# The output projections' weights of a two-layer trunk: split by two GpSimd transfers instead of a ScalarE copy and a VectorE subtraction

## Chip, cores and metric

One NeuronCore of a Trainium2 chip runs the whole kernel. The metric is device time in microseconds (us); each kernel was run several times and the median counts. Besides, one execution was taken by the hardware profiler; all rows below are from it.

## What is computed

Two residual layers on 256 tokens of width 1024, in float32. Layer 0 is a sparse attention mixer with three branches (compressed, selected, windowed), layer 1 a sliding-window attention with a sink. Cut to what matters here:

```python
for i in range(2):
    h = rms_norm(x, norm_gains[i])
    q, k, v, ..., z = split(h @ w_in)          # projections of the layer
    o = attention(q, k, v, ...)                # 16 heads of 64
    x = x + (o * silu(z)) @ w_out              # w_out: 1024 x 1024
```

The change concerns the last line of each layer, the product with `w_out` (`a_w_out` in layer 0, `b_w_out` in layer 1).

## The kernel before, in words

TensorE works in a reduced float32 format (F32R). To keep the accuracy of float32, each operand is written as a high part, its value rounded to F32R, and a low part, the value minus the high part. A product then takes three matmuls: high by high, high by low, low by high (`wh` and `wl` are the parts of a weight, `oz[h][:, 0]` and `oz[h][:, 1]` those of the gated attention output of token half h).

Every weight matrix is cut into pieces of 512 KB (128 partitions x 2 x 512 elements, or other shapes of nearly that size). `load_w` (L172) handles one piece: `load_raw` (L145) issues one transfer from HBM on SyncE's queue (L149) into a tile `wraw`; `split_w` (L152) then makes `wh` with a rounding copy (mostly on ScalarE, L141) and `wl` with a subtraction on VectorE (L169). There are five buffers each for `wraw`, `wh` and `wl`. `wraw` comes free as soon as the split is done; `wh` and `wl` only when the last matmul that reads the piece has run.

`out_proj` (L454) takes eight pieces of `w_out`, called (kk, n): kk is a quarter of the 1024 rows, n a half of the columns. Its order is written out (L462): first kk 0 to 2 for both n and both token halves h, then kk 3. Sums for n = 0 lie in the PSUM tiles `pya`, for n = 1 in `pyb`; the very last quarter of the output (layer 1, h = 1, n = 1) is cut in two, `pyb` and `tail`. Rows kk of `w_out` meet the heads of attention unit kk, so that the matmuls of kk can run as soon as unit kk is through with attention (`finish_unit`, L418); kk 3 waits for the last unit.

Nothing in the program fixes the order of the instructions across helpers: a planner puts each engine's instructions in order when the kernel is built, by a priority (program order, raised by `tc.high_priority(offset=...)`, which is HP = 200 for the splits) and by its own forecast of when operands and buffers are ready. So the pieces of `w_out` are loaded and split long before `out_proj` stands in the program, among the attention units, and its matmuls fill gaps of TensorE there. Each engine then works its list strictly in order.

GpSimd has work of its own that the attention waits for: in each unit the probabilities `p` are scaled by L71, eight instructions for h = 1 in layer 0, after VectorE has made their factor `rg`, and before TensorE transposes them (L447). The rest of GpSimd's work are sums of the rotary terms (L66), the gate (L405, L406) and small tables.

Of the kernel before, what the change touches and what calls it, by code (L numbers as in the profile page):

```python
# [20 lines left out]
F32 = mybir.dt.float32  # L21
F32R = mybir.dt.float32r
# [3 lines left out]
ALU = mybir.AluOpType  # L26
# [7 lines left out]
EPS = 1e-6  # L34
NEG = -1e30
HP, HPZ, HPS, HPT, HPQ, HPF = 200, 200, 0, 100, 250, 0
HPC, HPK = 300, 250
RSC, QLO = 'p', 'd'
WPS = ('d', 'd', 'd', 'd', 'd', 'd', 'd', 'd', 'd')
PHASES = (4, 13, 23, 29, 37, 43, 49, 55)  # L40
# [50 lines left out]
def tile_hybrid_trunk(ctx: ExitStack, tc: tile.TileContext, x, positions, norm_gains, a_w_in, a_cmp_pos,  # L91
                      a_cmp_w2, a_w_out, b_w_in, b_w_out, small, cmp_w1, out):
    nc = tc.nc
    pool = Pool(nc.gpsimd)
# [6 lines left out]
    wpool = ctx.enter_context(tc.tile_pool(name="wpool", bufs=NWHL))  # L101
# [8 lines left out]
    def banks(name, tag="acc"):  # L110
        return [bank(f"{name}{h}", tag) for h in range(2)]

    def mm(o, l, r, start, stop):
        nc.tensor.matmul(o, lhsT=l, rhs=r, start=start, stop=stop)  # L114
# [18 lines left out]
    nload, NLOW = [0], 4  # L133
# [5 lines left out]
    def copy_to(eng, dst, src):  # L139
        if eng == 'a':  # L140
            nc.scalar.activation(dst, src, AF.Copy)  # L141
        else:
            ENG[eng].tensor_copy(dst, src)

    def load_raw(w, k0, nk, c0, n, step=None):  # L145
        raw = wpool.tile([128, nk, n], F32, name="wraw", tag="wraw", bufs=NRAW)
        for k in range(0, nk, step or nk):
            ks = slice((k0 + k) * 128, (k0 + k + (step or nk)) * 128)
            nc.sync.dma_start(raw[:, k:k + (step or nk)], w[ks, c0:c0 + n].rearrange("(k p) n -> p k n", p=128))  # L149
        return raw  # L150

    def split_w(raw, step=None):  # L152
        wh = wpool.tile(list(raw.shape), F32R, name="wh", tag="wh")
        wl = wpool.tile(list(raw.shape), F32R, name="wl", tag="wl")
        with tc.high_priority(offset=HP if nload[0] >= NLOW else 0):
            hp_ = WHS[sum(nload[0] >= n for n in PHASES)]
            for k in range(0, raw.shape[1], step or raw.shape[1]):
                ks = slice(k, k + (step or raw.shape[1]))
                copy_to(hp_[nload[0] % len(hp_)], wh[:, ks], raw[:, ks])
            pat = WPS[sum(nload[0] >= n for n in PHASES)]  # L160
            eng = pat[nload[0] % len(pat)]
            nload[0] += 1
            cut = {'d': raw.shape[1], 'p': 0, 'b': raw.shape[1] // 2}[eng]
            cuts = [(nc.vector, slice(0, cut)), (pool, slice(cut, raw.shape[1]))]
            if step:
                cuts = [((nc.vector, pool)[k >= cut], slice(k, k + 1)) for k in range(raw.shape[1])]
            for e_, ks in cuts:
                if ks.stop > ks.start:
                    e_.tensor_tensor(wl[:, ks], raw[:, ks], wh[:, ks].bitcast(F32), op=ALU.subtract)  # L169
        return wh, wl  # L170

    def load_w(w, k0, nk, c0, n):  # L172
        return split_w(load_raw(w, k0, nk, c0, n))

    xt0 = work.tile([128, 2, D], F32, name="x", tag="big", bufs=1)
    xh = [xt0[:, h] for h in range(2)]
# [277 lines left out]
    def out_proj(oz, w, xt, sq_out, last):  # L454

        ws = {}
        pys = [banks("pya", "acc"), banks("pyb", "s")]
        acc = [[pys[n][h] for n in range(2)] for h in range(2)]
        KM = 3
        if last:  # L460
            tail = ps_a.tile([128, 256], F32, name="tail", tag="pz")
        order = [(kk, n, h) for n in range(2) for kk in range(KM) for h in range(2)]  # L462
        order += [(kk, n, h) for h in range(2) for n in range(2) for kk in range(KM, 4)]
        for kk, n, h in order:
            if (kk, n) not in ws:
                ws[kk, n] = load_w(w, 2 * kk, 2, 512 * n, 512)
            wh, wl = ws[kk, n]
            for k in range(2):
                sh, sl = oz[h][:, 0, 2 * kk + k, :], oz[h][:, 1, 2 * kk + k, :]
                if last and h == 1 and n == 1:  # L470
                    continue
                for i, (s, m) in enumerate(((sh, wh), (sh, wl), (sl, wh))):
                    mm(acc[h][n], s, m[:, k, :], kk == 0 and k == 0 and i == 0, kk == 3 and k == 1 and i == 2)
            if last and h == 1 and n == 1:

                for q in range(2):
                    for k in range(2):
                        sh, sl = oz[h][:, 0, 2 * kk + k, :], oz[h][:, 1, 2 * kk + k, :]
                        for i, (s, m) in enumerate(((sh, wh), (sh, wl), (sl, wh))):
                            mm(tail if q else acc[h][n][:, 0:256], s, m[:, k, 256 * q:256 * q + 256],  # L480
                               kk == 0 and k == 0 and i == 0, kk == 3 and k == 1 and i == 2)
            if kk == 3:
                sl_ = slice(512 * n, 512 * (n + 1))
                if last:
                    for c0, c1, src in (((512, 768, acc[h][n][:, 0:256]), (768, 1024, tail)) if h == 1 and n == 1
                                        else ((512 * n, 512 * n + 512, acc[h][n]),)):
                        nc.vector.tensor_tensor(xt[h][:, c0:c1], src, xt[h][:, c0:c1], op=ALU.add)
                        nc.sync.dma_start(outd[h * 128:(h + 1) * 128, c0:c1], xt[h][:, c0:c1])
                else:
                    nc.vector.tensor_tensor(xt[h][:, sl_], acc[h][n], xt[h][:, sl_], op=ALU.add)  # L490
                    sq = work.tile([128, 512], F32, name="xsq", tag="sq", bufs=1)
                    nc.scalar.activation(sq, xt[h][:, sl_], AF.Square, accum_out=sq_out[:, n, h:h + 1])
# [86 lines left out]
    def queries(n):  # L579
        acc = banks("aq")  # L580
        for kk in range(4):
            w = load_w(awi, 2 * kk, 2, 512 * n, 512)
            for h in range(2):
                proj(acc[h], hT, h, w, 2, 2 * kk)
        q_prep([heads(acc[h]) for h in range(2)], 0, qTs, 8 * n, r0, nrq0)

    with tc.tile_pool(name="cmp", bufs=1) as cp:
# [8 lines left out]
        for kk in range(4):  # L596
            w = split_w(first_w[kk], 1 if kk < FK else None) if kk < len(first_w) else load_w(awi, 6, 2, 1024, 512)
# [197 lines left out]
    sqs = work.tile([128, 2, 2], F32, name="sqs1", tag="sqs")  # L795
    xh = load_x("x1")
    out_proj(ozs, awo, xh, sqs, False)
    hT = work.tile([128, 2, 8, T], F32R, name="hT1", tag="hT", bufs=1)
    with tc.high_priority(offset=200):
# [73 lines left out]
    for step in 'q0 k0 z0 a0 q1 z1 a1 z2 a2 z3 a3'.split():  # L873
        {'q': queries1, 'k': lambda n: keys1(), 'z': zs1, 'a': attend1}[step[0]](int(step[1:]))
    out_proj(ozs, bwo, xh, None, True)


# [31 lines left out]
```

## Time and profile before

| | us |
|---|---|
| median of 3 runs | 289.76 (289.17 to 291.66) |
| the profiled execution's own time | 289.89 |
| its span, first to last instruction | 288.10 |
| outside of the span (289.89 less 288.10) | 1.79 |
| TensorE busy (share of the span) | 271.3 (94%) |
| VectorE busy | 221.1 (77%) |
| ScalarE busy | 184.2 (64%) |
| GpSimd busy | 124.3 (43%) |

Matmuls overlap in TensorE's pipeline, so that its 94% does not mean that it could take no more work. A chain of waits is the work that ended last, followed back step by step to what released it; time of an instruction counts for the end only where it is on that chain. In the rows PE is TensorE, PEld its weight loads, DVE VectorE, ACT ScalarE, POOL GpSimd, SP SyncE.

### The profile page before, as it was taken

Reading aid. Unit: us, or ns where it says so; the run is one execution under the profiler, and the core shown is the slowest. Engines: PE = TensorE matmul, PEld = TensorE weight load, DVE = VectorE, ACT = ScalarE, POOL = GpSimd, SP = SyncE. Lnnn points to the kernel's source line nnn. Section 1 sums busy time; section 2 is a strip of 40 time slices with the busy share of each in tenths; the row PEclk is TensorE's granted clock in tenths of the full one; section 3 lists DMA queues with packets and bytes.
Section 4 is the critical chain, followed back from the end, with each engine's and each line's share of the span. In section 5 each row is a group of like instructions: output and inputs, shape, how many; then the busy total and the mean of one; then the engine's idle time right before and its main releaser. Section 6 shows DMA issues by size and latency. Waiting matters only on the chain.

```text
span 288.1 us, 5292 instructions
## 1 busy us (share of the span) xinstructions
PE 271.3 (94%) x1772; PEld 229.1 (80%) x1772; DVE 221.1 (77%) x621; ACT 184.2 (64%) x441; POOL 124.3 (43%) x182
## 2 busy tenths in 40 slices
PE   5898999998999799998998999999999799999995
PEld 3667988877898797876776877789989799877874
DVE  3798847579769998988698284989969988784533
ACT  5491974365666767889688473547666949783620
POOL 7494514477720583636252500034394392253200
PEclk9799999999999999999999999999999989999999
DMA  7988769145527544221102354137774423100003
GB/s 224 306 265 262 256 224 245 49 138 147 146 75 200 165 149 146 76 74 36 39 0 75 147 167 127 47 99 220 221 213 154 141 78 104 45 2 0 1 2 146
DMA packets 33115, 37.52 MB, mean 130 GB/s; under 512 B 1680, under 2 KB 21568, under 8 KB 32960
## 3 DMA queue, kind: packets, MB, share of 16 engines
q1 hardware_dynamic: 33088, 37.18, 42.5%
q8 instruction: 14, 0.23, 0.3%
q14 instruction: 13, 0.11, 0.1%
HBM read 36.13 MB, written 1.05 MB: 129 GB/s over the span
## 4 chain that ended last, share of the span: by engine, by line
PE 71%; DVE 15%; ACT 5%; issue 3%; DMA 3%; SPq 1%; POOL 1%; ACTq 0%
PE pz L114 12%; PE po L114 8%; PE aqb L114 7%; PE pyb L114 6%; PE pya L114 6%; PE aq L114 5%; PE ptp L447 5%; DVE wl L169 4%; PE aks L114 4%; DMA wraw<-in_a_w_in_dram 3%; PE s L114 3%; PE avw L114 2%; PE sb L114 2%; DVE p L414 2%; PE akw L114 2%
## 5 line engine op out<-in xcount | busy, mean ns | idle before, releaser
L169 DVE TENSOR_TENSOR wl<-wraw,wh 128x1024 fp32r<-128x1024 f32 (+2 forms) x64 | 79.3, 1245 | 13.6 <-ACT wh L141 12.9
L141 ACT ACTIVATE wh<-wraw 128x1024 fp32r<-128x1024 f32 (+3 forms) x58 | 59.6, 1031 | 29.7 <-PE avw L114 4.9
L114 PE MATMUL pz<-hT,wh 128*128 128x256 f32 x256 | 50.3, 291 | 1.9 <-DVE zt L400 1.9
L114 PEld LDWEIGHTS pz<-hT,wh 128*128 128x128 f32 x256 | 41.4, 194 | 2.2 <-ACT sq L310 2.1
L114 PE MATMUL pz<-hT,wl 128*128 128x256 f32 x128 | 36.8, 287 | 0.0
L71 POOL TENSOR_SCALAR p<-p,rg 128x256 f32<-128x256 f32 (+1 forms) x48 | 22.9, 495 | 29.6 <-DVE rg L768 15.3
L416 ACT ACTIVATE p<-p,nm 128x128 f32<-128x128 f32 (+1 forms) x64 | 28.4, 447 | 4.9 <-DVE nm L414 4.7
L66 POOL TENSOR_TENSOR rt<-rt,rt 128x512 f32<-128x512 f32 (+2 forms) x14 | 21.3, 1530 | 23.8 <-DVE rt L324 23.8
L141 ACT ACTIVATE ptsb<-ptp 128x512 f32<-128x512 f32 x36 | 20.7, 586 | 10.4 <-PE ptp L447 10.4
L114 PEld LDWEIGHTS pz<-hT,wl 128*128 128x128 f32 x128 | 24.8, 194 | 0.0
L414 DVE CUSTOM_DVE_ANT_0 p<-s,mask,nrq 128x128 f32<-128x128 f32 (+1 forms) x64 | 24.2, 407 | 0.0
L114 PE MATMUL aqb<-wh,hT 128*128 128x512 f32 x64 | 21.3, 396 | 0.0
L114 PE MATMUL s<-kt,qT 128*128 128x272 f32 (+1 forms) x96 | 19.6, 305 | 1.6 <-DVE cwide L741 0.7
L114 PE MATMUL aq<-wh,hT 128*128 128x512 f32 x64 | 20.6, 393 | 0.0
L71 POOL TENSOR_SCALAR pb<-pb,rg 128x128 f32<-128x128 f32 (+1 forms) x24 | 13.8, 591 | 15.4 <-DVE rg L865 9.8
L414 DVE CUSTOM_DVE_ANT_0 pb<-sb,mask,nsink 128x128 f32<-128x128 f32 (+1 forms) x32 | 13.8, 471 | 5.1 <-PE ptp L447 3.9
L114 PEld LDWEIGHTS s<-kt,qT 128*128 128x128 f32 x96 | 14.5, 189 | 3.3 <-PE s L114 1.2
L447 PE MATMUL ptp<-identr,p 128*128 128x128 f32 x96 | 15.6, 277 | 1.5 <-ACT ptsb L141 1.4
L416 ACT ACTIVATE pb<-pb,nm 128x128 f32<-128x128 f32 (+1 forms) x32 | 14.2, 446 | 2.6 <-DVE nm L414 2.5
L114 PE MATMUL akc<-wh,hT 128*128 128x512 f32 x32 | 12.3, 451 | 3.0 <-ACT hT L280 1.2
L447 PEld LDWEIGHTS ptp<-identr,p 128*128 128x128 f32 x96 | 11.3, 140 | 3.6 <-ACT ptsb L141 2.1
L114 PEld LDWEIGHTS aq<-wh,hT 128*128 128x128 f32 x64 | 11.9, 188 | 2.5 <-ACT sq L310 0.2
(250 smaller groups left out, 689.5 us busy)
## 6 DMA issues: line engine op xcount, KB each, us to landing
wraw<-in_a_w_in_dram SPq DMA_DIRECT2D x25, 512.0 KB, 4.6
wraw<-in_b_w_in_dram SPq DMA_DIRECT2D x18, 512.0 KB, 4.3
wraw<-in_a_w_out_dram SPq DMA_DIRECT2D x8, 512.0 KB, 3.7
wraw<-in_b_w_out_dram SPq DMA_DIRECT2D x8, 512.0 KB, 4.0
x<-in_x_dram SPq DMA_DIRECT2D x4, 256.0 KB, 3.5
w<-in_cmp_w_dram SPq DMA_DIRECT2D x1, 1024.0 KB, 6.7
x<-in_x_dram SPq DMA_DIRECT2D x2, 512.0 KB, 3.8
wraw<-in_a_w_in_dram SPq DMA_DIRECT2D x2, 456.0 KB, 4.3
```

What stands on the lines that cost most here:

```text
L66: self.eng.tensor_tensor(out, a, b, op=op)
L71: self.eng.tensor_scalar(out, a, s0, s1, op0=op0, op1=op1)
L114: nc.tensor.matmul(o, lhsT=l, rhs=r, start=start, stop=stop)
L141: nc.scalar.activation(dst, src, AF.Copy)
L169: e_.tensor_tensor(wl[:, ks], raw[:, ks], wh[:, ks].bitcast(F32), op=ALU.subtract)
L414: nc.vector.tensor_tensor_reduce(out=p, in0=s, in1=mk, scale=nr, scalar=floor, op0=ALU.add, op1=ALU.min, accum_out=nm)
L416: nc.scalar.activation(p, p, AF.Exp, scale=-1.0, bias=nm, accum_out=total)
L447: nc.tensor.transpose(pt[:, i], s, ident)
```

## The change

`out_proj` calls a new function `load_parts` instead of `load_w`. For each of its 16 pieces (8 per layer) GpSimd issues three things: a transfer from HBM straight into `wh`, which rounds on its way since the target's type is F32R; an instruction that writes the negative of `wh` into `wl`; and a second transfer of the same 512 KB that is added to what `wl` holds. `wraw`, the copy on ScalarE and the subtraction on VectorE are gone for these pieces. The three are raised in priority by HPD = 250 in place of 200. The count `nload`, by which the engines of the other splits are chosen, still moves by one for each piece. All other weights stay as they were.

```diff
-HPC, HPK = 300, 250
+HPC, HPK, HPD = 300, 250, 250
@@
+    def load_parts(w, k0, nk, c0, n):
+
+        src = w[k0 * 128:(k0 + nk) * 128, c0:c0 + n].rearrange("(k p) n -> p k n", p=128)
+        wh = wpool.tile([128, nk, n], F32R, name="wh", tag="wh")
+        wl = wpool.tile([128, nk, n], F32R, name="wl", tag="wl")
+        with tc.high_priority(offset=HPD):
+            nload[0] += 1
+            nc.gpsimd.dma_start(wh, src)
+            pool.tensor_scalar(wl, wh.bitcast(F32), -1.0, 1.0, op0=ALU.mult, op1=ALU.mult)
+            nc.gpsimd.dma_start(wl, src, accum_op=ALU.add)
+        return wh, wl
@@ out_proj
             if (kk, n) not in ws:
-                ws[kk, n] = load_w(w, 2 * kk, 2, 512 * n, 512)
+                ws[kk, n] = load_parts(w, 2 * kk, 2, 512 * n, 512)
```

## Rows read from the trace of the kernel before

**Rows 1.** The page's head and its first part: busy us, share, instructions.

```profile
span 288.1 us, 5292 instructions
PE 271.3 (94%) x1772; PEld 229.1 (80%) x1772; DVE 221.1 (77%) x621; ACT 184.2 (64%) x441; POOL 124.3 (43%) x182
```

**Rows 2.** The page's chain that ended last, by engine, as shares of the span.

```profile
PE 71%; DVE 15%; ACT 5%; issue 3%; DMA 3%; SPq 1%; POOL 1%; ACTq 0%
```

**Rows 3.** Busy time by stretch (from:to, length, engines, PEclk, DMA share, GB/s).

```profile
95.00:118.00 23.00, 20.97 (x167) 19.37 (x166) 21.71 (x74) 16.98 (x47) 14.12 (x18) 1.00 0.43 139
...
137.00:166.00 29.00, 27.71 (x177) 21.81 (x178) 19.69 (x97) 19.97 (x65) 10.55 (x24) 1.00 0.19 63
...
227.00:251.00 24.00, 22.04 (x171) 20.42 (x170) 19.90 (x62) 18.06 (x55) 12.92 (x17) 0.93 0.28 88
251.00:285.00 34.00, 33.97 (x208) 27.00 (x206) 20.24 (x62) 16.88 (x49) 8.19 (x14) 1.00 0.05 17
```

**Rows 4.** The chain in order of time, 110 to 152 us (start, us, what).

```profile
116.67 1.16 DVE wl L169
...
120.41 1.14 DVE wl L169
...
133.21 1.38 DVE wl L169
...
148.86 0.95 ACT wh L141
```

**Rows 5.** Groups by shape: line, operation, count, busy us, mean ns, idle before.

```profile
L169 DVE TENSOR_TENSOR wl<-wraw,wh 128x1024 fp32r<-128x1024 f32 x59 | 74.4, 1267 | 11.9 <-ACT wh L141 11.3
L141 ACT ACTIVATE wh<-wraw 128x1024 fp32r<-128x1024 f32 x53 | 55.8, 1055 | 24.0 <-PE aks L114 3.9 <-PE pya L114 3.8 <-PE pz L114 3.6
```

**Rows 6.** Tile `wraw`: issue ns (min/median/max), first to last start; time to landing.

```profile
L149 SPq DMA_DIRECT2D wraw<-in_a_w_in_dram x30: 367/368/1556, 2.1 to 86.9; - x30
...
L149 SPq DMA_DIRECT2D wraw<-in_a_w_out_dram x8: 367/368/371, 88.7 to 111.9; - x8
...
DMA to landing us min/median/max: 3.0/4.1/8.7
```

**Rows 7.** VectorE in order of time: the splits of `w_out`, first and last per layer.

```profile
102.09 1.22 DVE L169 TENSOR_TENSOR wl<-wraw,wh 128x1024 fp32r<-128x1024 f32 x1
...
165.95 2.49 DVE L169 TENSOR_TENSOR wl<-wraw,wh 128x1024 fp32r<-128x1024 f32 x2
...
230.53 1.22 DVE L169 TENSOR_TENSOR wl<-wraw,wh 128x1024 fp32r<-128x1024 f32 x1
...
272.49 1.23 DVE L169 TENSOR_TENSOR wl<-wraw,wh 128x1024 fp32r<-128x1024 f32 x1 [1.93 <-ACT wh L141]
```

**Rows 8.** ScalarE in order of time: the last copy of each layer's `w_out`, its wait.

```profile
164.86 1.06 ACT L141 ACTIVATE wh<-wraw 128x1024 fp32r<-128x1024 f32 x1 [0.28 <-PE pya L114]
...
271.40 1.06 ACT L141 ACTIVATE wh<-wraw 128x1024 fp32r<-128x1024 f32 x1 [1.73 <-PE pyb L114]
```

**Rows 9.** TensorE in order of time: uses of those pieces, and its last matmul.

```profile
173.30 0.40 PE L114 MATMUL pyb<-wl,oz 128*128 128x512 f32 x1
...
280.88 0.39 PE L114 MATMUL pyb<-wl,ozb 128*128 128x512 f32 x1
...
284.69 0.28 PE L114 MATMUL tail<-wh,ozb 128*128 128x256 f32 x1
```

**Rows 10.** GpSimd in order of time (start, us, line, operation, idle before).

```profile
13.34 1.81 POOL L77 TENSOR_SCALAR wh<-wraw 128x1024 fp32r<-128x1024 f32 x1 [0.18 <-DMA wraw<-in_a_w_in_dram]
...
101.61 0.62 POOL L405 TENSOR_SCALAR zth<-zth 128x512 f32<-128x512 f32 x1 [3.92 <-ACT zth L401]
102.31 2.16 POOL L406 TENSOR_TENSOR zt<-zth,zt 128x512 f32<-128x512 f32 x1
...
113.90 4.89 POOL L71 TENSOR_SCALAR p<-p,rg 128x256 f32<-128x256 f32 x8 [4.40 <-DVE rg L768]
...
122.16 1.28 POOL L406 TENSOR_TENSOR zt<-zth,zt 128x512 f32<-128x512 f32 x1
```

## The prediction

> **What bounds the kernel now.** I read the page first. No engine is the plain bound: TensorE's 94% are busy time with overlapping matmuls, VectorE has 77%, ScalarE 64%, GpSimd 43% [rows 1]. So the next view is the chain that ended last: 71% TensorE, 15% VectorE, 5% ScalarE, 1% GpSimd [rows 2]. The reader should take from it that an edit which relieves VectorE and ScalarE can give back at most what lies on their fifth of the chain, and that GpSimd, which gets the new work, is nearly absent from it now.
>
> Then the stretches in which the splits of `w_out` run. In layer 0 the eight subtractions start between 102.09 and 165.95 us, in layer 1 between 230.53 and 272.49 us [rows 7]. VectorE is busy 21.71 of 23.00 us from 95 to 118, and 19.69 of 29.00 from 137 to 166; in layer 1 it is busy 19.90 of 24.00 from 227 to 251, and from 251 to 285 TensorE is busy 33.97 of 34.00 [rows 3]. So layer 0 has a VectorE that the attention queues for, and layer 1's end has TensorE in the way whatever the others do.
>
> The chain in order of time says which splits count. In layer 0 four pieces of it are splits of `w_out`: three subtractions of 1.16, 1.14 and 1.38 us and one copy of 0.95 us [rows 4], together 4.63 us. In layer 1, behind 230 us, the chain's long pieces hold no split of `w_out` at all; they are matmuls and transposes. The other twelve subtractions already hide behind TensorE.
>
> **What is removed.** 16 subtractions of 1.267 us are 20.3 us of VectorE, 16 copies of 1.055 us are 16.9 us of ScalarE [rows 5]; off SyncE's queue go 16 issues of 0.368 us [rows 6], which stood on no engine that computes. Of these 37 us only the 4.63 on the chain are sure to come off. Taking them off can't gain less than zero and, if VectorE's whole queue in layer 0 moves up, gives at most its eight subtractions, 8 x 1.267 = 10.1 us. I take 4.6: by the chain the rest is hidden by matmuls that stay.
>
> **What is added on GpSimd.** Each piece brings one negation and two issues. The nearest row for the negation is the rounding copy of the same shape on GpSimd, 1.81 us, from below twice the 0.62 us of the half-size one-input instruction, 1.24 [rows 10]; I take 1.5. No GpSimd issue is in the trace. On SyncE's queue one takes 0.37 us, at the longest 1.56 [rows 6]; these are my bounds, and I take 1.0, halfway between. So 3.5 us per piece, 28 us per layer. In layer 0 GpSimd is idle 8.9 us from 95 to 118 and 18.5 us from 137 to 166 [rows 3]; with the 19 us between them the 28 us fit, but they use up most of it. Cost on the chain: nothing, since the chain is only 1% GpSimd; the cover is TensorE's own work, the output projection's matmuls among it. If that cover is gone, what is late is the scaling of `p`, 4.89 us for eight instructions [rows 10], behind which transposes and the products with v wait.
>
> **What is added in waiting.** Before, a piece was in SBUF as `wraw` long ahead: layer 0's loads were issued from 88.7 to 111.9 us [rows 6]. Once a `wh` buffer came free the split took 1.06 + 1.27 = 2.3 us. Now the load itself needs the `wh` buffer, and the parts come one behind the other: issue 1.0, transfer, negation 1.5, issue 1.0, adding transfer. A load lands in 4.1 us in the median, 3.0 at best, 8.7 at worst [rows 6]; I take 4.0. The adding transfer has to read SBUF besides HBM: from 3.0 (as a fast load) to 8.2 (twice the median); I take 5.0, nearer to a load, because the bytes from HBM are the same and the DMA engines are busy only 0.05 to 0.43 there [rows 3]. That makes 12.5 us from free buffer to finished `wl`, with ends 8.0 (0.37 + 3.0 + 1.24 + 0.37 + 3.0) and 21.8 (1.56 + 8.7 + 1.81 + 1.56 + 8.2).
>
> Most pieces have that time, since only the last piece of a layer gets its buffer late. In layer 0 it was free at 164.86 (the copy had waited for a matmul into `pya`) [rows 8], so `wl` would be whole at 177.4; its first use was at 173.30 [rows 9]. The 4 us are covered by the last unit's products with v and by the h = 1 half of `out_proj`: nothing. In layer 1 the buffer came free at 271.40 [rows 8], `wl` is whole at 283.9, and its first use was at 280.88, the last matmul at 284.69 [rows 9]. That is 3.0 us late, with 3.8 us of matmuls behind it of which less than one needs this `wl`. If the planner lets them pass nothing is lost, if not 3.0. I take a third, 1.0. The rank of 250 in place of 200 changes nothing by itself, as the pieces are issued when a buffer is free.
>
> One rule of the Trainium skill speaks against the change: SBUF — State Buffer, section "SBUF: two separate sides", says that GpSimd writes the entries of its own transfers into SBUF and is locked out while VectorE runs a two-port instruction, so that a transfer of about 620 ns took about 3100. No transfer of GpSimd's is in this trace, so nothing here shows it. By that figure, 2.5 us more for each transfer, the last piece would come 5 us later still and the sum, an estimate, would be 1.7 to 5 us higher.
>
> DMA: Bandwidth & Descriptors, section "Anatomy of one DMA — SWDGE (gpsimd) path", fits 2.0 us plus bytes by 436 GB/s for a transfer from GpSimd, which is 3.2 us for 512 KB against the 4.1 of the rows. With it in both transfers the last piece would be 0.4 us late and not 3.0, and the sum, an estimate, 0.9 us lower.
>
> **The sum.** Against the profiled execution's own 289.89 us (0.13 above the median of the runs): 289.89 - 4.6 + 1.0 = 286.3 us.
>
> **The rivals.**
>
> *More than the chain shows.* With VectorE at 94% from 95 to 118 [rows 3], each subtraction pushes all that is queued behind it, and the chain shows only the push that happened to be last. Then all eight of layer 0 count: 289.89 - 10.1 + 1.0 = 280.8. Against it: from 251 TensorE has no gap, so what layer 0 gains must be kept through layer 1.
>
> *GpSimd's queue takes the place.* It works in order. A negation that waits for its transfer holds back the scaling of `p` behind it. One such meeting costs 1.5 to 3.5 us; if each of layer 0's units but the first meets one at 1.5, three of them give back 4.5 of the 4.6. Time 289.89 - 4.6 + 1.0 + 4.5 = 290.8. For it: most of GpSimd's idle time there is used up, and `p` waits on it in every unit. Against it: TensorE has the output projection to do meanwhile.
>
> *Slower: the last piece of layer 1 comes far too late.* If both transfers take some 8 us (near the 8.7 of the slowest load and twice the median [rows 6]), a piece needs 1.0 + 8 + 1.5 + 1.0 + 8 = 19.5 us and layer 1's last `wl` is whole at 290.9, 10.0 us after its use [rows 8, 9]. Up to 4 us of other matmuls may pass, so 6 to 10 us are lost; layer 0's last piece, 11 us late, has cover for about 9 and loses 2. Time 289.89 - 4.6 + 8 + 2 = 295.3. It decides from about 17 us per piece on, where 4.6 + 2.9 us are lost. For it: the same GpSimd instruction took 1.28 us once and 2.16 another time [rows 10], so GpSimd is held up by others at busy times, and two transfers in a row have not been tried in this kernel. The skill's rule on VectorE's lock, above, would work in this way. Against it: the DMA engines are nearly idle there.
>
> **How the numbers follow.** Forecast (284 to 288.5) 0.38; more than the chain shows 0.15; GpSimd's queue 0.21; late last piece 0.26. About 1% (2.9 us) is what a measurement of this kernel can tell from no change. Faster by over 1% means below 286.9: the second case and nearly three quarters of the first, 0.15 + 0.28 = 0.43. Within 1%: the rest of the first and most of the third, 0.10 + 0.19 = 0.29. Slower: the fourth and a little of the third, 0.28. The range reaches down to the second case, 281, and up into the fourth, 294.5, and leaves out something under 0.2, mostly above. The forecast's own range is 284 to 288.5.
>
> **What would show each step.** Right: no splits of `w_out` on VectorE and ScalarE, subtractions of this shape 59 - 16 = 43 [rows 5]; the stretch of layer 0's attention shorter by about 4 to 5 us; GpSimd's busy time up by some 50 us; in layer 1 the last `wl` matmul into `pyb` waits for a DMA by 1 to 3 us. Wrong: negations that start long after their load has landed, or idle TensorE until a GpSimd scaling of `p` (the third case); TensorE idle for 5 us or more before the last matmuls of either layer, with a DMA as releaser (the fourth); landing times of GpSimd's transfers outside of 3 to 8 us would move the sum by the steps above.

## The result and the profile after

The changed kernel takes 309.74 us in the median (308.79 to 310.66, 4 runs) against 290.71 for the kernel before on the same chip (289.17 to 291.98, 4 runs). The ratio is 1.066, with a 95% interval of 1.062 to 1.069. The prediction said 286.3 and at most 294.5.

First the page of the profile after: its head, the busy times (us, share of the span, instructions), the chain that ended last by engine, the queue of GpSimd's transfers (packets, MB, share of the 16 DMA engines' span) and the new issues (count, size, median us from issue to landing).

```profile
span 307.1 us, 5263 instructions
PE 278.5 (91%) x1772; PEld 232.9 (76%) x1772; DVE 214.7 (70%) x605; ACT 169.8 (55%) x425; POOL 167.0 (54%) x230
...
PE 49%; DMA 17%; DVE 15%; POOL 7%; ACT 5%; issue 4%; SPq 1%; DVEq 0%; POOLq 0%; ACTq 0%
...
q0 software_dynamic: 8704, 16.78, 27.0%
...
wh<-in_a_w_out_dram POOLq DMA_DIRECT2D x8, 512.0 KB, 5.2
wl<-in_a_w_out_dram POOLq DMA_DIRECT2D x8, 512.0 KB, 6.4
wh<-in_b_w_out_dram POOLq DMA_DIRECT2D x8, 512.0 KB, 6.9
wl<-in_b_w_out_dram POOLq DMA_DIRECT2D x8, 512.0 KB, 7.2
```

VectorE and ScalarE did get lighter. The totals of before stand in [rows 1]. Yet of the chain [rows 2] TensorE has only 49% instead of 71, while DMA went from 3% to 17 and GpSimd from 1% to 7. Transfers and GpSimd together have 24% of it, against 4% before, and these are the thing to look for in the chain in order of time (start, us, what):

```profile
112.74 4.54 DMA wh<-in_a_w_out_dram
117.35 1.05 POOL wl L71
...
164.67 5.41 DMA wh<-in_a_w_out_dram
...
171.50 6.37 DMA wl<-in_a_w_out_dram
177.92 1.43 PE pyb L114 x5
...
252.54 6.96 DMA wh<-in_b_w_out_dram
...
261.90 8.38 DMA wl<-in_b_w_out_dram
270.32 0.87 PE tail L114 x5
...
282.83 7.33 DMA wh<-in_b_w_out_dram
...
291.67 7.22 DMA wl<-in_b_w_out_dram
298.93 3.57 PE pyb L114 x10
302.50 1.08 PE tail L114 x5
```

Whole pieces now stand in it as they were asked for: load, negative, adding transfer, first matmul. Where before had four splits of about a microsecond [rows 4], the last piece of layer 1 alone has 16.1 us (282.83 to 298.89, the landing). The fourth piece of layer 1 stands on the chain too, with 17.7 us (252.54 to 270.28), but TensorE had other work for most of that time and stood for it 1.48 us.

Where in time it was lost is read from the matmuls of layer 1's gate, which begin after layer 0 is done. This is the tile view of `pz` from 150 us on, low parts (count, ns min/median/max, first and last start), of before and then of after:

```profile
L114 PE MATMUL pz<-hT,wl x64: 278/283/415, 200.8 to 250.7; 128*128 128x256 f32 x64
```

```profile
L114 PE MATMUL pz<-hT,wl x64: 277/283/415, 205.6 to 257.6; 128*128 128x256 f32 x64
```

Up to layer 1's gate 4.8 us are lost (205.6 against 200.8). From there to the end of the span before takes 288.1 - 200.8 = 87.3 us and after 307.1 - 205.6 = 101.5, which is 14.2 more. These two numbers, "to the gate" and "the rest", are given below for each experiment. Their sum is the difference of the spans. For e_neg_dve they are left out, since its profiled execution took 318.35 us and its three other runs 313.04 to 313.90.

### The profile page after: what moved, and what is told of

Read it like the earlier page. It is cut to its first block, busy times and chain, and to the rows that moved or that the text cites. A ratio compares the mean times of both kernels' runs of the same rounds, so it can differ in the third digit from the quotient of the medians.

```text
span 307.1 us, 5263 instructions
## 1 busy us (share of the span) xinstructions
PE 278.5 (91%) x1772; PEld 232.9 (76%) x1772; DVE 214.7 (70%) x605; ACT 169.8 (55%) x425; POOL 167.0 (54%) x230
## 3 DMA queue, kind: packets, MB, share of 16 engines
q0 software_dynamic: 8704, 16.78, 27.0%
## 4 chain that ended last, share of the span: by engine, by line
PE 49%; DMA 17%; DVE 15%; POOL 7%; ACT 5%; issue 4%; SPq 1%; DVEq 0%; POOLq 0%; ACTq 0%
PE pz L114 9%; DMA wl<-in_b_w_out_dram 5%; PE aq L114 5%; DMA wh<-in_b_w_out_dram 5%; DVE wl L169 4%; PE po L114 4%; PE aks L114 4%; PE aqb L114 4%; DMA wh<-in_a_w_out_dram 3%; PE ptp L459 3%; PE pya L114 3%; PE pyb L114 3%; PE s L114 2%; DMA wraw<-in_a_w_in_dram 2%; PE avw L114 2%
## 5 line engine op out<-in xcount | busy, mean ns | idle before, releaser
L169 DVE TENSOR_TENSOR wl<-wraw,wh 128x1024 fp32r<-128x1024 f32 (+3 forms) x48 | 60.0, 1257 | 13.2 <-ACT wh L141 12.8
L141 ACT ACTIVATE wh<-wraw 128x1024 fp32r<-128x1024 f32 (+3 forms) x42 | 42.7, 1022 | 28.5 <-PE pya L114 6.3
L114 PE MATMUL pz<-hT,wl 128*128 128x256 f32 x128 | 37.6, 294 | 0.0
L71 POOL TENSOR_SCALAR wl<-wh 128x1024 fp32r<-128x1024 f32 x16 | 17.6, 1098 | 23.5 <-DMA wh<-in_a_w_out_dram 12.7
L71 POOL TENSOR_SCALAR p<-p,rg 128x256 f32<-128x256 f32 (+1 forms) x48 | 21.7, 591 | 2.0 <-PE po L114 1.1
L114 PE MATMUL s<-kt,qT 128*128 128x272 f32 (+1 forms) x96 | 20.4, 312 | 1.0 <-DVE nm L426 0.6
L428 ACT ACTIVATE pb<-pb,nm 128x128 f32<-128x128 f32 (+1 forms) x32 | 14.2, 446 | 10.7 <-DVE nm L426 10.5
L459 PE MATMUL ptp<-identr,p 128*128 128x128 f32 x96 | 17.0, 283 | 2.6 <-POOL p L71 2.5
L71 POOL TENSOR_SCALAR tabc<-tabc,r 128x128 f32<-128x128 f32 x2 | 1.8, 890 | 27.5 <-DVE r L265 27.5
```

What stands on the lines that cost most here:

```text
L71: self.eng.tensor_scalar(out, a, s0, s1, op0=op0, op1=op1)
L428: nc.scalar.activation(p, p, AF.Exp, scale=-1.0, bias=nm, accum_out=total)
L459: nc.tensor.transpose(pt[:, i], s, ident)
```

## The experiments

Two theories ran through them. **Theory L**: a piece takes long from its issue to its finished low part, and the products wait for it. **Theory Q**: GpSimd works in order, and whatever stands behind its wait for a fresh transfer is late. The table has all runs; ratios are to the kernel before, with the 95% interval, and the last two columns come from the one profiled execution of each and are differences to before's 200.8 and 87.3 us.

| run | new load used for | median us | ratio (interval) | to the gate | the rest |
|---|---|---|---|---|---|
| after | all | 309.74 | 1.066 (1.062 to 1.069) | +4.8 | +14.2 |
| e_layer0_only | layer 0 | 300.11 | 1.035 (1.030 to 1.040) | +6.0 | +3.8 |
| e_layer1_only | layer 1 | 304.34 | 1.049 (1.045 to 1.053) | -0.4 | +14.8 |
| e_last_old | all but the last of each layer | 303.48 | 1.045 (1.039 to 1.050) | +5.2 | +7.9 |
| e_first_three | first three of each layer | 296.49 | 1.020 (1.017 to 1.023) | +6.0 | +1.1 |
| e_middle | three in the middle | 300.62 | 1.034 (1.028 to 1.040) | +3.4 | +6.1 |
| e_last_two | last two | 305.51 | 1.053 (1.047 to 1.060) | +5.2 | +7.8 |
| e_no_add | all, without the adding transfer | 297.04 | 1.024 (1.019 to 1.029) | +3.1 | +4.4 |
| e_noadd_neg_dve | the same, negative on VectorE | 293.81 | 1.011 (1.008 to 1.014) | +2.6 | +2.0 |
| e_two_loads | all, two loads and no negative | 292.13 | 1.006 (1.003 to 1.009) | -0.3 | +3.8 |
| e_plain_pool | none; GpSimd issues the old load | 293.67 | 1.012 (1.007 to 1.016) | +0.3 | +2.1 |
| e_ft_defer | first three, negatives held in layer 0 | 295.89 | 1.019 (1.013 to 1.025) | +1.0 | +4.5 |
| e_after_defer | all, the same held | 305.94 | 1.054 (1.049 to 1.058) | +1.2 | +15.9 |
| e_layer0_defer | layer 0, the same held | 297.32 | 1.025 (1.019 to 1.031) | +2.6 | +4.7 |
| e_own_bufs | all, own buffers for layer 1's last two | 305.72 | 1.055 (1.050 to 1.060) | +4.9 | +9.3 |
| e_hpd0 | all, rank 0 | 312.32 | 1.074 (1.069 to 1.078) | +5.2 | +18.1 |
| e_neg_dve | all, negative on VectorE | 313.60 | 1.078 (1.075 to 1.082) | not read | not read |
| e_p_dve | all, `p` scaled on VectorE | 322.72 | 1.111 (1.108 to 1.114) | +15.2 | +17.6 |
| b_p_dve | none, `p` scaled on VectorE | 297.60 | 1.025 (1.021 to 1.028) | +4.5 | +4.4 |

A caution on the last column: in e_layer0_only layer 1 runs the old code and still takes 3.8 us longer, so in another order of work a stage moves by some 4 us by itself. A difference of that size in that column alone proves nothing here. The column before it is steadier: with layer 0 as before it moved by -0.4 us (e_layer1_only).

### Which transfer it is

e_no_add leaves the adding transfer out, so that the low part is only the negative of the high one:

```diff
-            nc.gpsimd.dma_start(wl, src, accum_op=ALU.add)
```

> The second, adding transfer is left out, so that the low part is only the negative of the high part; all else as in the changed kernel. Theory L: a piece is ready 7 to 8 us sooner (the adding transfer lands 6.4 to 7.2 us behind its issue, and the issue takes 1.2), so the last piece of layer 1 is there near 290 and not 299 us: 298 to 302 us. If the adding transfer is the whole cause: 289 to 293 us. If GpSimd's queue is the cause, with negations that wait for the first transfer: 304 us or more, as those waits stay.

It took 297.04 us: of the 19 lost, 12.7 come back, and the other 6.4 stay. The loads land faster too, as its DMA issues and its queue show:

```profile
q0 software_dynamic: 4352, 8.39, 10.7%
...
wh<-in_a_w_out_dram POOLq DMA_DIRECT2D x8, 512.0 KB, 4.5
wh<-in_b_w_out_dram POOLq DMA_DIRECT2D x8, 512.0 KB, 4.1
```

e_two_loads keeps the number and size of the transfers, but takes away the negative and the order between them: both parts get the rounded weight, and the low part is not computed.

```diff
-            pool.tensor_scalar(wl, wh.bitcast(F32), -1.0, 1.0, op0=ALU.mult, op1=ALU.mult)
-            nc.gpsimd.dma_start(wl, src, accum_op=ALU.add)
+            nc.gpsimd.dma_start(wl, src)
```

> Each piece still moves 2 x 512 KB by two GpSimd transfers, but the second is a plain rounding load into the low part, and the negation is left out, so that neither waits for the other (the low part is then the weight itself, not the remainder). Without the adding transfer the loss was 6.4 us, with it 19. Theory C, it is the row of dependent steps (load, negation, adding transfer) in a five-buffer ring and in GpSimd's queue: both transfers go out as soon as the buffers are free, a piece is ready some 6 us after that, 291 to 295 us. Theory A, it is the adding transfer's own cost on the DMA engines or the second 512 KB per piece: 297 to 305 us, no better than leaving the second transfer out (297.0).

292.13 us, 0.6% over before. So it is not the bytes, nor the number of GpSimd's issues, that cost 19 us; it is that each step waits for the one ahead and that the second transfer adds. This run tells a second thing: all 16 subtractions and copies are gone from VectorE and ScalarE, and in the balance nothing was gained, at the gate (-0.3) no more than in all.

```profile
q0 software_dynamic: 8704, 16.78, 19.6%
```

e_plain_pool is the kernel before with one thing changed: GpSimd issues the loads of `w_out` into `wraw`.

```diff
-                ws[kk, n] = load_w(w, 2 * kk, 2, 512 * n, 512)
+                ws[kk, n] = load_pool(w, 2 * kk, 2, 512 * n, 512)
```

> The kernel before, with one thing moved: the loads of the output projections' pieces are issued by GpSimd as plain transfers into the same five raw buffers; splits on ScalarE and VectorE as before. It shows what issuing from GpSimd costs by itself. Theory L: nothing, 289 to 293 us, since raw buffers are free long ahead, whatever the landing time is. If transfers issued by GpSimd land late in themselves (the changed kernel's rounding ones took 5.2 and 6.9 us against 3.7 to 4.0 from SyncE), the plain ones land in 5 to 7 us here too; if it is the rounding, in 4. If the waits for buffers in GpSimd's queue hold up the attention: 295 us or more.

293.67 us, 1.2% more. Issuing from GpSimd has a small price of its own.

### Which pieces: parts of the change alone

```diff
-                ws[kk, n] = load_parts(w, 2 * kk, 2, 512 * n, 512)
+                ws[kk, n] = (load_w if last else load_parts)(w, 2 * kk, 2, 512 * n, 512)        # e_layer0_only
+                ws[kk, n] = (load_parts if last else load_w)(w, 2 * kk, 2, 512 * n, 512)        # e_layer1_only
+                ws[kk, n] = (load_w if (kk, n) == (3, 1) else load_parts)(w, 2 * kk, 2, 512 * n, 512)  # e_last_old
+                ws[kk, n] = (load_parts if n == 0 and kk < 3 else load_w)(w, 2 * kk, 2, 512 * n, 512)  # e_first_three
+                ws[kk, n] = (load_parts if n == 1 and kk < 3 else load_w)(w, 2 * kk, 2, 512 * n, 512)  # e_middle
+                ws[kk, n] = (load_parts if kk == 3 else load_w)(w, 2 * kk, 2, 512 * n, 512)            # e_last_two
```

> The two transfers only in layer 0's output projection; layer 1's eight pieces are split as before. In the changed kernel layer 1's first gate matmul starts at 205.5 us, in the kernel before at 200.7. Theory L with most of the loss at the end of layer 1: about 5 us above the kernel before, 295 to 296 us. If layer 0 also disturbs what follows: 299 us or more. If layer 0 by itself is a gain that is lost at its last piece: below 293 us.

> The new load in layer 1 only, layer 0 by the old load and split. In the profiled executions layer 1 from its first gate matmul to the end took 101.5 us with the change and 87.3 before. If these 14.2 us are layer 1's own late pieces: 303 to 306 us. If a part of them comes from a layer 0 that ran in another order (layer 1's old code took 91.1 behind layer 0's new load): 299 to 302 us.

> As the changed kernel, but the last piece of each layer, (3, 1), is loaded and split in the old way (SyncE load, ScalarE copy, VectorE subtraction); the other 14 pieces stay with the two GpSimd transfers. Theory L, the last piece's two transfers in a row come after its buffer is free and TensorE stands still: in the changed kernel the last piece of layer 1 is issued at 282.8 us and its low part is there at 298.9, and the last piece of layer 0 has 13.3 us of transfers and negation at 164.7 to 177.9. Then this run gives back about 11 us in layer 1 and 2 to 4 in layer 0: 295 to 298 us. Theory Q, GpSimd's instructions wait behind the negations and issues in its queue all along: at most 4 us come back, 305 us or more.

> The new load only for the first three pieces of each layer, which are asked for during the attention and have the most time to spare; the other five of each layer by the old load and split. Theory L (the loss is pieces that come too late behind a gate, in the output projections themselves): 290 to 293 us, no slower than before by over 1%. Theory Q (each wait of GpSimd's costs, wherever it stands): 294 to 298 us.

> The new load only for the three middle pieces of each layer (rows 0 to 767 of the second half of the columns); the other five by the old load and split. The first three alone cost 5.9 us, and leaving the very last alone gave back 6. If the cost of the pieces adds up, the middle three cost 5 to 8 us: 296 to 299 us. If the middle ones are free (they have a ring's turn of time to spare): 290 to 293 us.

> The new load only for the last two pieces of each layer, those with nothing behind them to cover a late landing. Theory L (a piece takes 15 us from issue to landing and the end waits for it): 296 to 300 us. If the last pieces are late only because the six before them fill GpSimd's queue: 290 to 294 us.

Layer 1 alone costs 13.7 us and layer 0 alone 9.5, of which 6.0 stand at the gate. So layer 1's loss is its own: +14.8 in the rest with layer 0 untouched. The last piece of each layer is worth 6.3 us, less than theory L had expected of it (295 to 298). The three groups of pieces cost 5.9, 9.9 and 14.8 us alone, some 30 together where the whole change costs 19. The costs of single pieces don't add up. e_middle and e_last_two also came out above what either theory had given them (at most 299 and 300 us).

The first three were the miss that told most. They are asked for during the attention, with the most time to spare, and theory L had them free at 290 to 293 us. Here is GpSimd in order of time in that run (start, us, instruction, idle before and its releaser):

```profile
99.39 0.96 POOL L182 DMA_DIRECT2D wh<-in_a_w_out_dram  x1 [1.24 <-PE s L114]
104.60 1.04 POOL L71 TENSOR_SCALAR wl<-wh 128x1024 fp32r<-128x1024 f32 x1 [4.24 <-DMA wh<-in_a_w_out_dram]
105.62 0.61 POOL L417 TENSOR_SCALAR zth<-zth 128x512 f32<-128x512 f32 x1
...
117.72 1.05 POOL L71 TENSOR_SCALAR wl<-wh 128x1024 fp32r<-128x1024 f32 x1 [2.45 <-DMA wh<-in_a_w_out_dram]
118.75 4.62 POOL L71 TENSOR_SCALAR p<-p,rg 128x256 f32<-128x256 f32 x8
```

GpSimd stands for 4.24 and 2.45 us until its own load has landed. Behind it `zth` goes from 101.61 to 105.62 us and the eight scalings of `p` from 113.90 to 118.75 [rows 10]. This is theory Q in the rows, at the very place where the prediction had put a cost of nothing.

### Holding the negatives behind GpSimd's other work

In e_ft_defer the factor -1 of layer 0's first three negatives is made from the scaled `p` of the first and the second unit, so that GpSimd can't reach them earlier. Transfers and negatives stay the same.

```diff
+            if g == 0:
+                pm = ps[3][:, (PSC0, PSC1)[h].index('p')].rearrange("p b t -> p (b t)")
+                pool.tensor_scalar(hold[:, h:h + 1], pm[:, 0:1], 0.0, -1.0, op0=ALU.mult, op1=ALU.add)
...
-            pool.tensor_scalar(wl, wh.bitcast(F32), -1.0, 1.0, op0=ALU.mult, op1=ALU.mult)
+            pool.tensor_scalar(wl, wh.bitcast(F32), -1.0 if l1[0] else hold[:, k0 > 0:(k0 > 0) + 1], 1.0, op0=ALU.mult, op1=ALU.mult)
```

> The new load for the first three pieces of each layer only, as in the run at 296.5 us, but in layer 0 the negative of the first piece is held until GpSimd has scaled the first unit's p, those of the second and third until it has scaled the second unit's (a tiny GpSimd instruction makes the factor of -1 out of that p). The transfers, negatives and adding transfers are the same; only GpSimd's waits for fresh transfers move behind its other work. Theory Q (layer 0's loss is GpSimd standing for the loads ahead of zth and of the eight p scalings): the first product of layer 0's output projection starts near 119 us instead of 125.1, layer 1's gate near 202 us instead of 206.5, and the whole takes 290 to 293 us. Theory L (the pieces are late by their length): as late or later, 296 to 300 us.

GpSimd in the same stretch:

```profile
99.25 0.97 POOL L182 DMA_DIRECT2D wh<-in_a_w_out_dram  x1 [1.23 <-PE s L114]
101.73 0.62 POOL L418 TENSOR_SCALAR zth<-zth 128x512 f32<-128x512 f32 x1 [1.50 <-ACT zth L414]
...
110.63 1.13 POOL L71 TENSOR_SCALAR wl<-wh,hold 128x1024 fp32r<-128x1024 f32 x1
...
113.25 3.94 POOL L71 TENSOR_SCALAR p<-p,rg 128x256 f32<-128x256 f32 x8
```

The wait is gone, `zth` and `p` start when they did before, and of the 6.0 us at the gate 5.0 come back. The whole gained only 0.6 us (295.89 against 296.49), since the rest went from +1.1 to +4.5. So theory Q's time at the gate came as expected, and its time at the end did not. To see whether it holds with all eight pieces loaded the new way, the same hold was put into the whole change and into its layer 0:

> The whole change, with the negatives of layer 0's first three pieces held behind GpSimd's p scalings of the first and the second unit (as in the run with the first three pieces alone, where that gave back 5.0 us by layer 1's gate and 0.6 of the whole). Theory Q (GpSimd's early waits are layer 0's loss): layer 1's first gate matmul at 201 to 203 us instead of 205.6, and the whole 304 to 307 us. Theory L (layer 0's loss is its last pieces, 13 us from issue to whole): the gate still at 205 to 207, the whole 308 to 312 us.

> The new load in layer 0 only, with the first three negatives held as above; layer 1 by the old load and split. Without the hold this took 300.1 us, with the gate of layer 1 at 206.8. Theory Q: gate at 201 to 203 us and the whole 294 to 296. Theory L: gate at 205 to 207 and the whole 299 to 302.

305.94 us and a gate at +1.2 in the first: 3.6 of the 4.8 us back at the gate and 3.8 in all. In the second the gate went from +6.0 to +2.6 and the time from 300.11 to 297.32, between the two theories' numbers. GpSimd's early waits are the larger part of what layer 0 loses up to the gate (3.6 of 4.8 us, 3.4 of 6.0); 1.2 to 2.6 us of that are left. In all, the hold gave back 2.8 of the 9.5 us of e_layer0_only, and the rest behind the gate stays unexplained.

### Who makes the negative, and in which rank

```diff
-            pool.tensor_scalar(wl, wh.bitcast(F32), -1.0, 1.0, op0=ALU.mult, op1=ALU.mult)
+            nc.vector.tensor_scalar(wl, wh.bitcast(F32), -1.0, 1.0, op0=ALU.mult, op1=ALU.mult)     # e_neg_dve; without the adding transfer e_noadd_neg_dve
...
-HPC, HPK, HPD = 300, 250, 250
+HPC, HPK, HPD = 300, 250, 0       # e_hpd0
```

> The adding transfer is left out, so the low part is only the negative of the high part, and that negative is made by VectorE instead of GpSimd. Only GpSimd's issue of the rounding loads and a wait of VectorE for them remain. Theory Q (GpSimd's in-order waits for a transfer hold its p scalings and its next issues, and that is the 6.4 us that remained without the adding transfer): 291 to 294 us. Theory V (a wait for a fresh transfer costs the same on whichever engine makes the negative, since its own work stands behind it): 296 to 300 us.

> The whole change, but the negative is made by VectorE (the trace of before has 128x1024 subtractions there at about 1.4 us). GpSimd now waits only where it issues the adding transfer. Theory Q (GpSimd's in-order wait for the rounding load is a large share of the loss): 300 to 305 us. Theory L (the length of the chain load, negative, adding transfer is the loss; who makes the negative matters little): 307 to 313 us.

> The whole change with the rank of its three steps among the work of their engine set to 0 instead of 250, so that the loads and negatives are put later in GpSimd's order and the p scalings earlier. If being put too early in GpSimd's queue (scalings behind the wait) is the loss: 300 to 306 us. If being late is the loss: 310 to 318 us, the last pieces landing later still.

Without the adding transfer, taking the wait off GpSimd gives back 3.2 of the 6.4 us, as theory Q had it. With it, VectorE makes it worse, 313.60: then VectorE stands for the load, and GpSimd still stands for VectorE ahead of its adding issue (that this is how it loses is argued, not shown). Rank 0 makes the pieces later still, 312.32; its last load went out at 286.35 us. Neither of the two ranks is free.

e_p_dve tried the reverse: `p` is scaled by VectorE, so that none of it stands behind GpSimd's waits, and b_p_dve does the same to the kernel before.

```diff
-PSC0 = 'dp'
-PSC1 = 'pp'
-PSL = 'pppd'
+PSC0 = 'dd'
+PSC1 = 'dd'
+PSL = 'dddd'
```

> As the changed kernel, but all scalings of the attention's probabilities run on VectorE, so that none stands behind a negation or an issue in GpSimd's queue. To be read against the kernel before with the same move. Theory Q, the scalings behind GpSimd's waits cost about 6 us in layer 0 and in layer 1: the distance between the two is 19 less 4 to 8, so 11 to 15 us. If GpSimd's queue costs nothing: 18 us or more.

> The kernel before with all scalings of the probabilities on VectorE, the control of the other run with this move. VectorE gets 60 more instructions of 0.3 to 0.5 us where it is busy 68 to 94% of the time: 293 to 302 us.

The distance grew to 25.1 us (322.72 - 297.60). This doesn't clear the queue: the pieces still wait there one after the other, and the last of layer 1 was asked for late and took as long.

```profile
296.99 7.17 DMA wh<-in_b_w_out_dram
...
305.67 7.07 DMA wl<-in_b_w_out_dram
312.78 3.57 PE pyb L114 x10
```

### Why layer 1's last piece is asked for so late

GpSimd of the changed kernel at layer 1's end, in order of time:

```profile
273.45 0.74 POOL L182 DMA_DIRECT2D wh<-in_b_w_out_dram  x1 [0.67 <-PE pya L114]
...
278.98 1.47 POOL L71 TENSOR_SCALAR pb<-pb,rg 128x256 f32<-128x256 f32 x3 [3.58 <-DVE rg L877]
280.42 1.04 POOL L71 TENSOR_SCALAR wl<-wh 128x1024 fp32r<-128x1024 f32 x1
281.76 1.22 POOL L184 DMA_DIRECT2D wl<-in_b_w_out_dram  x1 [0.30 <-POOL wl L71]
282.83 0.91 POOL L182 DMA_DIRECT2D wh<-in_b_w_out_dram  x1
290.32 1.05 POOL L71 TENSOR_SCALAR wl<-wh 128x1024 fp32r<-128x1024 f32 x1 [6.57 <-DMA wh<-in_b_w_out_dram]
291.67 1.22 POOL L184 DMA_DIRECT2D wl<-in_b_w_out_dram  x1 [0.30 <-POOL wl L71]
```

The last load stands behind the adding issue of the piece ahead, and that behind its negative. The load of the piece ahead went out at 273.45, when a matmul into `pya` had freed its buffer, and took 6.2 us to land (tile view), so that its negative could start at 279.6 at the earliest. The scalings, which wait 3.58 us for VectorE, held it only 0.8 us longer, to 280.42. So the last load goes out at 282.83, one piece behind. The view shows no wait for a buffer ahead of it, but a wait that ended while the issue ahead still ran would not be seen there. Before, the copy of the last piece had its buffer at 271.40 [rows 8]. TensorE then stands, by the waits view (us in total, times, longest):

```profile
PE pyb L114 <- DMA wl<-in_b_w_out_dram: 5.7, 1, 5.7
```

e_own_bufs gives layer 1's last two pieces buffers of their own, in the space of `hT`, so that they wait for no matmul:

```diff
+                own = None
+                if last and kk == 3:
+                    if n == 0:
+                        wx = work.tile([128, 4, 2, 512], F32R, name="wx", tag="hT", bufs=1)
+                    own = (wx[:, 2 * n], wx[:, 2 * n + 1])
```

> As the changed kernel, but in layer 1 the last two pieces, (3, 0) and (3, 1), get buffers of their own (the space of the layer's input hT, free after the last gate matmul near 257 us), so that their transfers no longer wait for a ring buffer, which came free at 273.4 and 282.8 us. Splitting the last piece the old way gave back 6 us. Theory L: the ring is what makes them late, and 8 to 12 us come back in layer 1: 298 to 302 us. If GpSimd's queue and the adding transfers of the earlier pieces set the pace there: 304 us or more.

Its layer 1 lost 9.3 us instead of 14.2, so a free buffer is only part of it. Now the queue was full before that: by stretch, GpSimd is busy 27.81 of 34 us and the DMA engines 0.92 (length, engines' busy time, PEclk, DMA share, GB/s), and the adding transfer that ended last, now that of a piece without a buffer of its own, took 9.30 us.

```profile
251.00:285.00 34.00, 31.10 (x211) 24.76 (x210) 18.42 (x62) 16.57 (x56) 27.81 (x38) 1.00 0.92 186
...
278.01 9.30 DMA wl<-in_b_w_out_dram
287.36 1.42 PE pyb L114 x5
```

No run beats the kernel before. With e_two_loads at best equal, though it leaves the low parts out, there was little to win by relieving VectorE and ScalarE in this way.

## Why the prediction was wrong

**The gain of 4.6 us wasn't there.** This step failed. It took the four splits on the chain [rows 4] for time that would come off. e_two_loads takes off all 16 splits, and layer 1's gate comes 0.3 us earlier, not 4.6. Of before's chain the splits were the last releaser; that with them gone other work was there at about the same time is argued, not shown. e_two_loads has a price of its own: 32 issues on GpSimd, loads that wait for `wh` and `wl` buffers, and from 95 to 118 us a granted clock of 0.93, where before has 1.00 [rows 3]. VectorE is relieved there, 18.61 us against 21.71, but TensorE is busy as long as before, 20.93 us against 20.97 (columns as in [rows 3]):

```profile
95.00:118.00 23.00, 20.93 (x157) 19.73 (x157) 18.61 (x74) 13.35 (x44) 17.46 (x24) 0.93 0.69 206
```

So no gain was left in any run, and how much was made and lost again is open. In the profile after 43 subtractions of this shape are left of 59, as the prediction said, and VectorE's share of the chain is 15% as before.

**The instructions on GpSimd were sized well, their place was not.** Negatives took 1.10 us in the mean (taken 1.5, lower end 1.24), the issues 0.89 and 0.77 (layers 0 and 1) for the load and 1.22 for the adding one in the median (taken 1.0): about 3.1 us per piece instead of 3.5. GpSimd's busy time rose by 42.7 us (forecast some 50). The failed step is "cost on the chain: nothing". It counted idle time against busy time and left out that GpSimd, in order, waits in the middle of a piece. (Of the 19 us that it added between its two stretches, GpSimd was busy 8.71.) The waits are in the page of after, in the last part of this row (count, busy us, mean ns, idle before it):

```profile
L71 POOL TENSOR_SCALAR wl<-wh 128x1024 fp32r<-128x1024 f32 x16 | 17.6, 1098 | 23.5 <-DMA wh<-in_a_w_out_dram 12.7
```

Priced as a rival, at 4.5 us, this came close: holding three negatives gives back 3.6 us at the gate. The mechanism was right and the nearness of the number in part luck, as the rival had three meetings at 1.5 us, and GpSimd stood six times in layer 0, for 12.7 us, of which 4.8 at most came through to layer 1's gate. In the prediction it was one of two cases to choose from, and it came in addition.

**The waiting per piece was a bit too short.** By the medians loads took 5.2 and 6.9 us (taken 4.0) and adding transfers 6.4 and 7.2 (taken 5.0). The last pieces took 13.2 us in layer 0 (164.67 to 177.87) and 16.1 in layer 1 (taken 12.5), inside the ends of 8.0 and 21.8. The 16.1 is even under the 17 from which the slower rival was to decide.

**The start of layer 1's last piece is where most went.** The prediction let its load go out at 271.40, when its buffer came free [rows 8], and had `wl` whole at 283.9. It was whole at 298.9, 15.0 us later: 11.4 from the issue (282.83) and 3.6 from the length. Of the 11.4 us 4.8 are layer 0's, by which all of layer 1 began later; 6.6 are layer 1's own. The step treated the last piece as if it were alone. The eight pieces of a layer go through one in-order queue, each of about 12 to 20 us from its load's issue to its last landing (15 to 19 in layer 1) and with two dependent steps in it, and the pieces of layer 1 come close together: from 251 to 285 us the transfers raised the DMA engines' share from 0.05 [rows 3] to 0.76 and GpSimd's busy time from 8.19 to 25.38 us, as this stretch of after shows (columns as in [rows 3]), and behind it TensorE is busy 12.89 of 22 us.

```profile
251.00:285.00 34.00, 31.89 (x215) 25.54 (x215) 18.75 (x62) 17.38 (x57) 25.38 (x36) 1.00 0.76 148
285.00:307.00 22.00, 12.89 (x64) 9.88 (x60) 5.52 (x10) 0.90 (x2) 2.27 (x2) 0.84 0.46 114
```

So where the prediction took 1.0 us for the tail, layer 1 lost 14.2; e_layer1_only shows 14.8 with layer 0 untouched. The rows place some 9.5 of the 14.2: TensorE stands 5.67 us for the last piece and 1.48 for the fourth, and about 2.3 are the lower clock of the last matmuls (an estimate from the row in the last section). Where the other 4.7 went is not shown; the stage moved by nearly as much, 3.8, with its own code unchanged. The argument that the DMA engines are nearly idle there, used against the slower rival, was read from a trace that did not yet have the transfers in it.

**Layer 0's last piece was not quite hidden.** It was whole at 177.87, as forecast (177.4), and the first matmul with it stood on the chain at 177.92. TensorE stood 0.60 us for it. Its price is at most the 1.2 us that remain at the gate in e_after_defer, and in e_last_two, alone and in another order, up to 5.2.

**The rivals and the range.** The slower rival named the right wait (the last piece of layer 1, with TensorE idle and a DMA as releaser, seen for 5.7 us), at 295.3 us; the queue rival named the right loss in layer 0. Both came true, and the range had them as alternatives. Added up, and with no gain, their prices give 289.89 + 4.5 + 10 = 304.4 us, against 308.79 in the profiled execution. The slower rival had 8 us of its 10 in layer 1, where 14.2 were lost.

**What stays open.** Layer 1's 14 us are shared by the length of the pieces (without the adding transfer 4.4 are left), the buffer (own buffers give back 4.9) and the queue. These overlap, and the runs don't split them further. Nor do they say why layer 1's old code takes 3.8 us longer behind a changed layer 0.

The Trainium skill's rule that was weighed against the change (SBUF — State Buffer, section "SBUF: two separate sides": GpSimd is locked out of writing its transfers' entries while VectorE runs a two-port instruction, so that a transfer of about 620 ns took about 3100) doesn't show here: with VectorE busy 77% of the span, e_plain_pool's transfers landed after 4.1 and 4.4 us in the median. Those of SyncE in [rows 6] have 4.1. No row tells which of VectorE's instructions are two-port ones, so this doesn't refute the rule.

## What to carry to other kernels

A split of a load into dependent steps on an in-order engine is priced by three things and not by its busy time: what stands behind each wait on that engine, how many such pieces stand in a row there, and when the first step can go out in the new order. The chain of waits says which work ended last, not how much time comes back when it goes; leaving the work out in a trial run (here two plain loads) tells what is left of it, with the price of what stands in its place. Rivals that work in different stages are added up, not chosen from.

## What the runs showed of the hardware

A transfer that adds into SBUF is dearer than its bytes. In the changed kernel 512 KB landed after 6.2 us at the fastest and 6.5 in the median, where a rounding load from the same queue took 4.1 to 4.5 (e_no_add). The loads beside it are slower too, 5.2 and 6.9 in the median; the last one, issued 1.07 us behind an adding transfer, took 7.3. By the queue's share of the 16 DMA engines, 16.78 MB took 0.270 x 307.1 = 83 us with the adding transfers and 0.196 x 291.6 = 57 us as plain rounding loads.

GpSimd's issue of an adding transfer held the engine for 1.22 us in the median, that of a load for 0.73 at the least.

When TensorE had stood for 5.7 us, its first matmul took 0.80 us, twice the 0.39 of [rows 9], which are its two clock levels; the granted clock of the whole stretch was 0.84. The matmuls behind it, up to the last, ran at a granted clock of 0.50, the lower level, so that of their 4.7 us about half, 2.3 (an estimate from the two levels), is the clock's. So a wait at the very end costs more than its length. TensorE after, in order of time, and the stretch by its busy times (columns as in [rows 3]):

```profile
298.93 0.80 PE L114 MATMUL pyb<-wl,ozb 128*128 128x512 f32 x1 [5.67 <-DMA wl<-in_b_w_out_dram]
...
298.90:303.60 4.70, 4.64 (x15) 3.86 (x15) 1.12 (x2) 0.00 (x0) 0.00 (x0) 0.50 0.12 47
```

VectorE did not get as much lighter as its subtractions. Those of the shape 128x1024 went from 74.4 us [rows 5] to 55.1, the engine as a whole only from 221.1 [rows 1] to 214.7. Other instructions on it grew longer, the scaling of `p` most plainly: the same 16 took 0.32 us each before and 0.44 after (groups by line: count, busy us, mean ns, idle before).

```profile
L773 DVE TENSOR_SCALAR p<-p,rg 128x128 f32<-128x128 f32 x16 | 4.1, 316 | 0.0
```

```profile
L785 DVE TENSOR_SCALAR p<-p,rg 128x128 f32<-128x128 f32 x16 | 5.9, 443 | 0.0
```

In e_two_loads they took 0.33. e_no_add and e_noadd_neg_dve differ only in the engine that makes the negatives, GpSimd in the first and VectorE in the second, and there they took 0.42 and 0.33:

```profile
L784 DVE TENSOR_SCALAR p<-p,rg 128x128 f32<-128x128 f32 x16 | 5.6, 415 | 0.0
```

```profile
L784 DVE TENSOR_SCALAR p<-p,rg 128x128 f32<-128x128 f32 x16 | 4.2, 333 | 0.0
```

So the longer scalings come with GpSimd's negatives. By what way GpSimd's work slows VectorE's is not shown.
